# A decoder trunk's matmuls in groups of eight and of four columns: the groups of four are placed elsewhere behind the heads' products and at the begin of a step

## The chip, the cores and the metric

One NeuronCore of a Trainium2 chip runs the whole kernel. The metric is the device time of one execution in microseconds, as the median of several runs. Engines are named as in the profile: PE is TensorE (matmuls; PEld its weight loads), DVE is VectorE, ACT is ScalarE, POOL is GpSimd, SP is SyncE.

## What is computed

The reference is a decoder trunk with one layer (`DEPTH = 1`), for 256 rows of 4096 in float32: RMSNorm, stick-breaking attention with 32 heads of 128 and a SiLU gate, the residual, and a last RMSNorm.

```python
proj = rms_norm(x, norm_attn) @ w_in          # (256, 4096) @ (4096, 16384): q, k, v, gate
q, k, v, g = split(proj)
z = q @ k.T / sqrt(128)                       # per head, strictly causal
log_a = log_sigmoid(z) + suffix_sum(log_sigmoid(-z))
o = exp(log_a) @ v
h = x + (o * silu(g)) @ w_out                 # (256, 4096) @ (4096, 4096)
return rms_norm(h, final_norm)
```

The two projections are nearly all of the work.

## The kernel before

**Units and steps.** The columns of the two projections are taken in 20 units, one after the other: units 0 to 15 for `w_in`, each with the q, k, v and gate columns of two heads, and units 16 to 19 for `w_out`. A unit has 16 steps; step `s` brings 256 of the 4096 rows of the contraction. A step multiplies two halves of the rows of x (or of the heads' output), 128 each, by two halves of the contraction and two blocks of 512 weight columns. That would be eight products of 128x128 by 128x512; steps 1, 2, 4, 5, 7, 8, 10, 11, 13 and 14 of most units form them with seven, from sums and differences of the blocks (`SEVEN`, line 46, `SEVEN_PARTS`, line 83), the others and all steps of the units 0 and 16 with eight. The results add up in PSUM in up to seven banks over a unit, and `combine` (line 708) makes the columns of them at its end.

**Triples.** Each product is in float32 by three matmuls: high by high, high by low, low by high, where an operand's high part is its rounding to the narrower type that TensorE multiplies (`fp32r`) and the low part is the rest. I call the three a triple. There are 2386 triples, 7158 matmuls, in a fixed order (the list `order`). ScalarE makes the high parts of the weights (`wh`), VectorE the low parts (`wl`) and the sums; the weights come in by DMA, issued by SP and for some sums by GpSimd with an addition on the way.

**Groups of columns.** A matmul reads 512 columns of its moving operand and writes 512 of a PSUM bank. It doesn't go through them from the first to the last: the 512 are cut into short groups that lie side by side, and each of four rounds takes every fourth group. A letter for each matmul of a triple says how long a group is, `e` for eight columns and `c` for four. An `e` reads columns 0 to 7, 32 to 39, 64 to 71 and so on in its first round, a `c` 0 to 3, 16 to 19, 32 to 35. The moving operand and the bank are cut alike, so the result is the same in either order.

```python
ROUNDS = 4                                                   # line 35
RUNS = {"e": 8, "c": 4}
BEHIND_OTHERS = ("ccc", "ecc")
IN_STEP = ("cce", "ecc", "ccc")
...
for k, (x, y) in enumerate(((ah, bh), (ah, bl), (al, bh))):  # mm3, line 812
    to, y = (t.rearrange("p (h q e) -> p q h e", q=ROUNDS, e=RUNS[orders[k]]) for t in (out_, y))
...
orders = "eee"                                               # product, line 1237
if since_others < len(BEHIND_OTHERS):
    orders = BEHIND_OTHERS[since_others]
elif p["i"] == 0 and k == 0:
    orders = IN_STEP[p["s"] % len(IN_STEP)]
since_others += 1
```

So a triple is `eee` unless it is one of the first triples behind the heads' products, or the first of its step. In the kernel before, step 0 (3, 6, ...) begins with `cce`, step 1 (4, 7, ...) with `ecc`, step 2 (5, 8, ...) with `ccc`.

**The heads' products.** The attention of the two heads of unit `u` runs while unit `u + 1` is multiplied. A head puts five small pieces of work between the triples (`head`, line 823, and the function behind it): the transposes of its q and k (four matmuls), the scores (five), the scan (four, with 384 columns first), the transposes of the gate (two), and the product with v (four). That makes 160 places where TensorE leaves the triples. Each is issued by `ten` (line 344), which sets the counter `since_others` to zero, so the triples behind it are counted from there. Ahead of the scan stand the scores of the same head by some 30 matmuls of the projection; in between ScalarE makes `f` of the scores `z`, and `fh`, and VectorE `fl`.

**The order of the work.** It is laid down when the program is built. The class `Plan` (line 112) plays the kernel through with a cost for each instruction (a triple counts 666 ns whatever its letters) and issues the instructions of each engine in the order that comes out. So nearly all instructions carry line 131 in the profile, the line of the helper that records them; they are told apart by their tiles. `acc<-wh,sh` is a matmul into a bank with the stationary operand `sh` (from x; `oh` from the heads' output) and the weights' part `wh`; `sl`, `ol` and `wl` are low parts. The letters don't show in the profile; which triple a matmul belongs to follows from its place in the order.

Of the kernel before, what the change touches and what calls it, by code (L numbers as in the profile page):

```python
# [33 lines left out]

ROUNDS = 4
RUNS = {"e": 8, "c": 4}
BEHIND_OTHERS = ("ccc", "ecc")
IN_STEP = ("cce", "ecc", "ccc")
WARM, IDLE = 10, 640


# [206 lines left out]
def kernel(  # L248
# [988 lines left out]
    def product(n, k):  # L1237
# [4 lines left out]
        orders = "eee"  # L1242
# [5 lines that stand above are left out]
# [89 lines left out]
```

## Time and profile before

| | before |
|---|---|
| median of 3 runs | 1713.17 us (1711.64 to 1714.27) |
| profiled execution | 1711.9 us, its span 1710.2 us |
| granted TensorE clock, mean | 0.996 |
| PE busy | 1690.5 us, 7776 matmuls |
| DVE busy | 1608.5 us (94%) |
| ACT busy | 1202.4 us (70%) |
| matmuls of the triples | 7158, of them 1471 in groups of four |

How to read it: the profile is one execution, and its times count from the first instruction of the span. The duration of a matmul in the timeline (0.38 us and more) overlaps the next one's; what one costs is seen from one start to the next. A row of the timeline gives start, duration, engine, line, operation and tiles; a row ends with `x2` where two instructions of one kind were merged. A row of the view by stretches gives the stretch, its length, the busy time of TensorE, the matmuls touched, the granted clock, the DMA share and GB/s.

### The profile page before, as it was taken

To read this page: it belongs to the slowest core of one execution; us is meant where nothing else is said; L and a number is where in the kernel's file an instruction comes from. 1 tells how busy PE (TensorE), PEld (TensorE's weight loads), DVE (VectorE), ACT (ScalarE), POOL (GpSimd) and SP (SyncE) were. 2 spreads that over 40 slices of the span, in tenths; PEclk is the share of its full clock that TensorE was granted. 3 is DMA by queue.
4 is the path that set the end of the run, shared out by engine and by line. 5 is a ranking of instruction groups with operands and counts; after the bars stand their busy time and mean duration, and the time that the engine had idled before them with its cause. 6 is when DMAs were issued, how large, how long until landed. Compare 5 with 4: busy or idle time off the path is not lost. (4 is left out here: it accounts for less than half of the span.)

```text
span 1710.2 us, 25109 instructions
## 1 busy us (share of the span) xinstructions
PE 1690.5 (99%) x7776; PEld 1416.8 (83%) x7776; DVE 1608.5 (94%) x2025; ACT 1202.4 (70%) x1633; POOL 325.7 (19%) x400
## 2 busy tenths in 40 slices
PE   9999999999999999999999999999999999999996
PEld 7888888888888888888888888888888888888785
DVE  8889999999999999999999999999999987999996
ACT  8986767676767676767676768676767765656564
POOL 0012222122222222221212121222222112122110
PEclk9999999999999999999999999999999999999998
DMA  9978887978787979787979797878788977889794
GB/s 350 326 196 245 228 246 219 253 212 259 206 266 196 271 195 274 195 270 201 264 205 260 208 256 214 249 215 247 224 240 230 290 248 234 256 240 280 208 307 174
DMA packets 248439, 412.78 MB, mean 241 GB/s; under 512 B 28016, under 2 KB 72560, under 8 KB 248304
## 3 DMA queue, kind: packets, MB, share of 16 engines
q1 hardware_dynamic: 194544, 354.24, 62.2%
q0 software_dynamic: 53472, 56.65, 20.4%
q8 instruction: 61, 1.00, 0.2%
q14 instruction: 74, 0.61, 0.1%
q10 hardware_dynamic: 288, 0.28, 0.0%
HBM read 402.93 MB, written 8.13 MB: 240 GB/s over the span
## 5 line engine op out<-in xcount | busy, mean ns | idle before, releaser
L131 ACT CAST wh<-raw 128x1024 fp32r<-128x1024 f32 (+1 forms) x989 | 918.9, 970 | 371.7 <-PE acc L131 169.8
L131 DVE TENSOR_TENSOR wl<-raw,wh 128x1024 fp32r<-128x1024 f32 (+1 forms) x815 | 975.5, 1218 | 64.1 <-ACT wh L131 27.7
L131 PE MATMUL acc<-wh,sh 128*128 128x512 f32 x2048 | 775.9, 391 | 1.1 <-ACT wh L131 1.1
L131 PE MATMUL acc<-wh,sl 128*128 128x512 f32 x1898 | 729.1, 384 | 0.9 <-DVE sl L131 0.9
L131 PE MATMUL acc<-wl,sh 128*128 128x512 f32 x1748 | 670.1, 383 | 0.2 <-DVE wl L131 0.2
L131 POOL DMA_DIRECT2D raw<-in_w_in_dram x300 | 259.1, 958 | 1029.3 <-DMA raw<-in_w_in_dram 367.2
L131 PEld LDWEIGHTS acc<-wh,sh 128*128 128x128 f32 x2048 | 384.2, 188 | 79.5 <-DVE qk_sb L131 4.9
L131 PEld LDWEIGHTS acc<-wh,sl 128*128 128x128 f32 x1898 | 355.8, 187 | 68.5 <-DVE sl L131 1.5
L131 PEld LDWEIGHTS acc<-wl,sh 128*128 128x128 f32 x1748 | 328.3, 188 | 56.0 <-DVE wl L131 0.5
L131 DVE TENSOR_TENSOR raw<-raw,raw 128x512 f32<-128x512 f32 x348 | 237.2, 685 | 2.5 <-DMA raw<-in_w_in_dram 0.4
L131 PE MATMUL acc<-wh,oh 128*128 128x512 f32 x512 | 193.3, 385 | 0.6 <-DVE gv_sb L131 0.6
L131 PE MATMUL acc<-wh,ol 128*128 128x512 f32 x488 | 187.5, 384 | 0.0
L131 PE MATMUL acc<-wl,oh 128*128 128x512 f32 x464 | 178.6, 385 | 2.7 <-DVE wl L131 2.7
L131 DVE TENSOR_TENSOR wh<-raw,wh 128x512 fp32r<-128x512 f32 x174 | 119.2, 685 | 1.1 <-ACT wh L131 0.7
L131 DVE TENSOR_TENSOR raw<-raw 128x512 f32<-128x512 f32 x174 | 118.9, 683 | 0.0
L131 PEld LDWEIGHTS acc<-wh,oh 128*128 128x128 f32 x512 | 96.4, 188 | 18.4 <-DVE gv_sb L131 0.9
L131 PEld LDWEIGHTS acc<-wh,ol 128*128 128x128 f32 x488 | 91.9, 188 | 16.6
L131 PEld LDWEIGHTS acc<-wl,oh 128*128 128x128 f32 x464 | 87.4, 188 | 19.6 <-DVE wl L131 3.9
L131 POOL DMA_DIRECT2D raw<-in_w_out_dram x48 | 41.5, 970 | 181.1 <-DMA raw<-in_w_out_dram 67.5
L131 ACT ACTIVATE f<-f 128x384 f32<-128x384 f32 x96 | 50.4, 525 | 3.0
L131 POOL DMA_DIRECT2D p<-spill x27 | 17.6, 694 | 86.8 <-DVE ol L131 49.8
L131 DVE SCALAR_TENSOR_TENSOR gv_sb<-acc,scalars,gv_sb 128x512 f32<-128x512 f32 x45 | 33.5, 744 | 0.0
(83 smaller groups left out, 753.9 us busy)
## 6 DMA issues: line engine op xcount, KB each, us to landing
raw<-in_w_in_dram SPq DMA_DIRECT2D x1024, 256.0 KB, 4.4
raw<-in_w_out_dram SPq DMA_DIRECT2D x256, 256.0 KB, 4.2
raw<-in_w_in_dram POOLq DMA_DIRECT2D x300, 128.0 KB, 5.1
p<-spill POOLq DMA_DIRECT2D x27, 256.0 KB, 4.2
raw<-in_w_out_dram POOLq DMA_DIRECT2D x48, 128.0 KB, 5.0
xr<-in_x_dram SPq DMA_DIRECT2D x16, 256.0 KB, 5.3
xres<-in_x_dram SPq DMA_DIRECT2D x16, 256.0 KB, 5.4
out_dram<-h SPq DMA_DIRECT2D x16, 256.0 KB, 2.9
```

Of the source, the lines that this page charges most:

```text
L131: return self.tc.keep_in_program_order(getattr(self.engine, name)(*args, **kw))
```

## The change

Two constants are altered, and nothing else:

```diff
-BEHIND_OTHERS = ("ccc", "ecc")
-IN_STEP = ("cce", "ecc", "ccc")
+BEHIND_OTHERS = ("ccc", "ecc", "eee", "cce", "eee", "eee", "ecc")
+IN_STEP = ("cce", "ecc")
```

Behind the heads' products the first two triples keep their letters. The third is `eee` even where a step begins, the fourth is `cce`, the fifth and sixth are `eee` even where a step begins, and the seventh is `ecc`. A step that begins later than that starts with `cce` if its number is even and with `ecc` if it is odd; before, the three kinds went round by the step's number. By the code, of the 7158 matmuls 1515 are then in groups of four, in place of 1471. 82 triples turn from `eee` to `cce` behind the heads' products; of the 98 triples that were `ccc` at a step's begin none stays so, but for those that are also the first behind the heads' products.

## The prediction

> **What bounds the kernel now.** I read the page first, then the list of waits for TensorE alone, then the busy time by stretches, and last the timeline of TensorE around single steps. The profiled execution took 1711.9 us, 1710.2 of them its span.
>
> ```profile
> span 1710.2 us, 25109 instructions
> ...
> PE 1690.5 (99%) x7776; PEld 1416.8 (83%) x7776; DVE 1608.5 (94%) x2025; ACT 1202.4 (70%) x1633; POOL 325.7 (19%) x400
> ...
> PEclk9999999999999999999999999999999999999998
> ```
>
> The reader is to see that TensorE is busy from end to end at full clock. The waits agree: the longest entry among those of TensorE is this one, 2.9 us in 4 waits, one of them 2.2 us.
>
> ```profile
> PE acc L131 <- DVE wl L131: 2.9, 4, 2.2
> ```
>
> So TensorE sets the time, and the change alters nothing but the order in which its matmuls read their columns. The question is what one matmul costs. Three neighbouring steps of unit 0, 24 matmuls each, show it: step 7 (`ecc`), step 8 (`ccc`), step 9 (`cce`). Columns: stretch, its length, busy time, matmuls touched, granted clock, DMA share, GB/s.
>
> ```profile
> 45.31:50.59 5.28, 5.28 (x25) 1.00 1.04 378
> 50.59:56.10 5.51, 5.51 (x26) 1.00 0.72 233
> 56.10:61.42 5.32, 5.32 (x26) 1.00 0.96 336
> ```
>
> Step 7 is 5.28 / 24 = 0.220 us a matmul, step 8 is 0.2296, at the same clock and with TensorE never idle. The groups of instructions in the first two stretches show the same in the mean duration of one matmul, 382 against 390 ns:
>
> ```profile
> L131 PE MATMUL acc<-wh,sl 128*128 128x512 f32 x9 | 3.4, 382 | 0.0
> ...
> L131 PE MATMUL acc<-wh,sl 128*128 128x512 f32 x9 | 3.5, 390 | 0.0
> ```
>
> Only the first three matmuls of step 8 are in groups of four; the other 21 are in groups of eight, as in step 7, and still take 0.23. So the triple wholly in fours does not cost by itself: it puts TensorE into a **wide stretch** of about 0.230 us a matmul, which lasts until a later pair of fours (the `cce` of step 9: 5.32, 0.04 over 24 times 0.220) brings back the **narrow stretch** of 0.220. I count every term below as wide minus narrow. One matmul then carries 0.0096 us, and 1 us of gain is about 104 matmuls.
>
> **The change part by part.** By the code, no instruction is added or removed: 2386 triples stay where they are, and of 7158 matmuls those in fours go from 1471 to 1515. No DMA, wait or queue moves. (The change's words say that the fourth and seventh triple carry one product in groups of four; in the diff `cce` and `ecc` carry two, and I go by the diff.) Steps now begin with `cce` (even) or `ecc` (odd) unless fewer than seven triples lie behind the heads' products. A pair in a narrow stretch costs nothing in step 7 above. The eight steps 8 to 15 of unit 6, 177 matmuls, begin at the first of these rows and end at the second:
>
> ```profile
> 561.22 0.38 PE L131 MATMUL acc<-wh,sh 128*128 128x512 f32 x1
> ...
> 600.24 0.38 PE L131 MATMUL acc<-wh,sh 128*128 128x512 f32 x1
> ```
>
> 39.02 less 177 x 0.220 = 0.08 us, for five pairs and three `ccc`. I take 0.007 for a pair (ends 0 and 0.013) and 0.02 for a `ccc` that leaves the stretch narrow.
>
> *Unit 0.* Steps 1 to 15 run from the first row to the second:
>
> ```profile
> 13.30 0.38 PE L131 MATMUL acc<-wh,sh 128*128 128x512 f32 x1
> ...
> 93.64 0.60 PE L131 MATMUL tr<-ident,qk_sb 128*128 128x128 f32 x4
> ```
>
> 80.34 less 360 x 0.220 = 1.14 us too much; four of its five `ccc` (steps 5, 8, 11, 14) start a wide stretch. After: 15 pairs, 0.10. Gain 1.04.
>
> *Step 5 of units 2 to 15.* It has 18 matmuls ahead of a head's scan, begins with `ccc`, and is wide each time; the first and the last of the 14:
>
> ```profile
> 206.67 0.38 PE L131 MATMUL acc<-wh,sh 128*128 128x512 f32 x1
> ...
> 210.80 0.34 PE L131 MATMUL z<-fh,neg_tri 128*128 128x384 f32 x1
> ...
> 1305.98 0.38 PE L131 MATMUL acc<-wh,sh 128*128 128x512 f32 x1
> ...
> 1310.10 0.34 PE L131 MATMUL z<-fh,neg_tri 128*128 128x384 f32 x1
> ```
>
> 4.125 less 18 x 0.220 = 0.165. It is now the seventh triple and gets `ecc`: 0.007. Gain 14 x 0.158 = 2.2.
>
> *Step 1.* Here the third triple behind the scores is the step's `ecc`, and what follows is wide up to the scan, 24 matmuls, in 12 of the units 2 to 15; the first and the last:
>
> ```profile
> 184.38 0.39 PE L131 MATMUL acc<-wh,sh 128*128 128x512 f32 x1
> ...
> 189.88 0.33 PE L131 MATMUL z<-fh,neg_tri 128*128 128x384 f32 x1
> ...
> 1283.66 0.39 PE L131 MATMUL acc<-wh,sh 128*128 128x512 f32 x1
> ...
> 1289.16 0.33 PE L131 MATMUL z<-fh,neg_tri 128*128 128x384 f32 x1
> ```
>
> 5.50 less 5.28 = 0.22. After the change that third triple is `eee`. The same heads' product of the second head has an `eee` there already. In unit 6 its third triple begins at the first row, the fourth at the second, step 5 at the third:
>
> ```profile
> 542.26 0.39 PE L131 MATMUL acc<-wh,sh 128*128 128x512 f32 x1
> ...
> 542.96 0.38 PE L131 MATMUL acc<-wh,sh 128*128 128x512 f32 x1
> ...
> 544.94 0.38 PE L131 MATMUL acc<-wh,sh 128*128 128x512 f32 x1
> ```
>
> The third triple takes 0.70 (0.04 over), the nine matmuls behind it 1.98, which is narrow. So an `eee` there recovers by itself. What the new `cce` does to the fourth triple, directly behind such a third, no row shows. Its ends: nothing, or a wide stretch up to the pair of the seventh, nine matmuls at 0.0096 and 0.04 to end it, 0.13. I take 0.02, nearer to nothing, because the recovery is over at 542.96. Together 0.04 + 0.02 + two pairs, 0.08; gain 12 x 0.14 = 1.7.
>
> *Unit 16 and the last unit.* Unit 16's step 8 is the first two rows (5.51, 0.23 over); its step 14 is alike and half of step 2 is. In the last unit, step 14 and the step behind it, 45 matmuls, run from the third row to the fourth.
>
> ```profile
> 1408.87 0.38 PE L131 MATMUL acc<-wh,oh 128*128 128x512 f32 x1
> ...
> 1414.38 0.39 PE L131 MATMUL acc<-wh,oh 128*128 128x512 f32 x1
> ...
> 1670.93 0.38 PE L131 MATMUL acc<-wh,oh 128*128 128x512 f32 x1
> ...
> 1681.16 0.38 PE L131 MATMUL acc<-wh,oh 128*128 128x512 f32 x1
> ```
>
> 0.56 and 10.23 - 9.90 = 0.33; less the pairs, 0.5 and 0.3.
>
> *The other `ccc` at a step's begin.* Some 61 that stay narrow become pairs: 61 x 0.013 = 0.8.
>
> *What is added behind the heads' products.* 82 triples go from `eee` to `cce` and 50 (of `eee` or `ccc`) to `ecc`, of which 24 are counted in step 1 and 14 in step 5; 32 other third triples lose their pair. (94 - 32) x 0.007 = 0.4 lost. Also, how the first two triples behind a scan run depends on what ran ahead of it. Behind step 2's `ccc` six matmuls take 1.38 us (first two rows), behind the wide step 5 they take 1.43 (last two):
>
> ```profile
> 528.63 0.44 PE L131 MATMUL acc<-wh,sh 128*128 128x512 f32 x1
> ...
> 530.01 0.38 PE L131 MATMUL acc<-wh,sh 128*128 128x512 f32 x1
> ...
> 549.58 0.44 PE L131 MATMUL acc<-wh,sh 128*128 128x512 f32 x1
> ...
> 551.01 0.38 PE L131 MATMUL acc<-wh,sh 128*128 128x512 f32 x1
> ```
>
> The first may lose 0.05 and the second gain it, 14 times each: I take nothing, ends -1.4 and +1.4.
>
> **Sum:** 1.04 + 2.2 + 1.7 + 0.5 + 0.3 + 0.8 - 0.4 = 6.1 us off the profiled 1711.9, so 1705.8. The median of the runs, 1713.17, lies 1.3 above that execution; from it 1707.1.
>
> What hides behind TensorE must also be early enough. In unit 6 VectorE ends the second head's `fl` at 547.44 and the scan that reads it begins at 549.06: 1.6 us in hand, against 0.165 taken.
>
> ```profile
> 546.89 0.55 DVE L131 TENSOR_TENSOR fl<-f,fh 128x384 fp32r<-128x384 f32 x1
> ...
> 549.06 0.34 PE L131 MATMUL z<-fh,neg_tri 128*128 128x384 f32 x1
> ```
>
> The one long wait is near the end, where the chain of waits (first two rows) runs through the loads and VectorE:
>
> ```profile
> 1582.43 2.81 DMA raw<-in_w_out_dram
> ...
> 1588.98 2.28 DVE wl L131 x2
> ...
> 1591.30 0.80 PE L131 MATMUL acc<-wl,oh 128*128 128x512 f32 x1 [2.19 <-DVE wl L131]
> ...
> 1591.00:1596.00 5.00, 4.70 (x14) 0.66 0.99 297
> ```
>
> It costs 2.2 us and a clock of 0.66 behind it. A gain made long before moves that whole stage forward; only what units 17 and 18 gain (under 0.3 us) could be lost there.
>
> [...]
>
> **The rivals.**
> *Cost goes by the number of fours.* Each four costs 0.0096 wherever it stands; 44 more are 0.4 us: 1713.6. For it: the wide steps begin with the most fours. Against: step 7 has two fours and costs 5.28, and 21 eights of step 8 are wide. [...] Chance 0.05.
> *The gain becomes a wait.* TensorE reaches the heads' products sooner and waits there for VectorE and ScalarE; the 3.9 us of steps 1 and 5 are lost, 2.2 stay: 1711.0. Against: the 1.6 us in hand. Chance 0.07.
> *The fourth triple's pair starts a wide stretch, and the seventh's doesn't end it* (slower). Three heads' products a unit have six or more triples behind the fourth, 45 places in units 1 to 15; 24 wide matmuls each, up to the next step's begin, cost 0.23: 10.4 lost against 6.1, 1717.5. It decides from 0.14 us a place, 14 wide matmuls. For it: step 1 shows that a pair at the wrong place behind the heads' products does just this. Against: there the pair stood a triple earlier, before the recovery. Chance 0.06.
> The forecast has 0.82.
>
> **The numbers.** 1707.1 us. The unknown costs (a pair 0 to 0.013 at some 220 places, the fourth triple, the triples behind a scan) make 3 us to the good and 4 to the bad if all fall one way; they are independent, so I take half, 4 to 7.6 us of gain. With 1.3 us for the spread of the runs (1711.64 to 1714.27) to either side the forecast's own range is 1704 to 1710.5. Up to 1711 it takes in most of the second rival. A measurement tells 0.2%, 3.4 us, from no change: faster 0.82, within 0.12, slower 0.06.
>
> **What would show it.** In the profile after: steps 5, 8, 11 and 14 of unit 0 at 5.28 to 5.30 each; step 5 of units 2 to 15 at 3.96 to 3.98 ahead of the scan; step 1 at 5.31 to 5.40; TensorE's matmuls of `acc` some 6 us less in all, with the same waits. I am wrong if step 1 stays at 5.5, if a step that begins with a pair out of a narrow stretch turns wide, or if TensorE's waits grow by microseconds.

## The result, and the profile after

The kernel after takes 1708.36 us (median of 9 runs, 1706.34 to 1710.01); the kernel before, run beside it, takes 1711.86 (9 runs, 1710.44 to 1714.27). The ratio is 0.9976, with a 95% interval of 0.9967 to 0.9984: **faster by 0.24%, some 4.1 us**. The profiled execution took 1706.34 us against 1711.9.

The head of the page after (span, busy time, granted clock) and the longest wait of TensorE:

```profile
span 1704.6 us, 25109 instructions
...
PE 1685.6 (99%) x7776; PEld 1415.9 (83%) x7776; DVE 1607.4 (94%) x2025; ACT 1202.5 (71%) x1633; POOL 325.0 (19%) x400
...
PEclk9999999999999999999999999999999999999998
```

```profile
PE acc L131 <- DVE wl L131: 2.8, 4, 2.1
```

TensorE's busy time fell by 4.9 us (1690.5 to 1685.6) and its waits are as before: 4 waits for `wl`, 2.8 us, one of them 2.1. So nothing that was gained was lost again by waiting.

**The steps of unit 0.** Steps 7, 8 and 9 by stretches, in the kernel after (the first two columns are the stretch and its length; then the busy time of PE, PEld, DVE, ACT and POOL, each with the instructions touched; then the granted clock, the DMA share and GB/s):

```profile
45.29:50.59 5.30, 5.30 (x26) 4.50 (x24) 4.90 (x8) 5.24 (x11) 0.00 (x0) 1.00 1.00 364
50.59:55.88 5.29, 5.29 (x25) 4.50 (x24) 4.55 (x8) 4.75 (x11) 0.00 (x0) 1.00 0.75 222
55.88:61.17 5.29, 5.29 (x25) 4.50 (x24) 4.85 (x10) 5.26 (x13) 0.00 (x0) 1.00 0.94 310
```

Step 8 was 5.51 and is 5.29. Steps 1 to 15 run from the first of the next rows to the second, 79.40 us against 80.34:

```profile
13.55 0.38 PE L131 MATMUL acc<-wh,sh 128*128 128x512 f32 x1
...
92.95 0.38 PE L131 MATMUL tr<-ident,qk_sb 128*128 128x128 f32 x2
```

**Step 5 of unit 6,** from its first matmul to the scan, in the kernel after:

```profile
543.55 0.38 PE L131 MATMUL acc<-wh,sh 128*128 128x512 f32 x1
...
547.51 0.34 PE L131 MATMUL z<-fh,neg_tri 128*128 128x384 f32 x1
```

3.96 us against 4.12 before, and 3.96 is 18 x 0.220; the other 13 units show the same 3.96.

**Step 1,** in two neighbouring units of the kernel after. Three rows each: the third triple behind the scores (the step's begin), the fourth, and the scan. First unit 5, then unit 6:

```profile
436.93 0.39 PE L131 MATMUL acc<-wh,sh 128*128 128x512 f32 x1
...
437.59 0.38 PE L131 MATMUL acc<-wh,sh 128*128 128x512 f32 x1
...
442.23 0.34 PE L131 MATMUL z<-fh,neg_tri 128*128 128x384 f32 x1
```

```profile
521.20 0.39 PE L131 MATMUL acc<-wh,sh 128*128 128x512 f32 x1
...
521.90 0.39 PE L131 MATMUL acc<-wh,sh 128*128 128x512 f32 x1
...
526.73 0.34 PE L131 MATMUL z<-fh,neg_tri 128*128 128x384 f32 x1
```

Unit 5 takes 5.30, unit 6 takes 5.53, no less than before. They part at the third triple. In unit 5 it takes 0.66, three narrow matmuls, and the pair of the fourth does no harm. In unit 6 it takes 0.70, and everything from there to the scan is wide; step 1 at 5.5 was one of the prediction's own signs of being wrong. Over the units 2 to 15, eight are like unit 6 (2, 4, 6, 7, 9, 11, 13, 15) and six like unit 5. This is the step that did not come as forecast.

**A part that is not the change's.** The last matmul of the triples starts 5.56 us earlier than before (first row before, second after):

```profile
1696.82 0.39 PE L131 MATMUL acc<-wh,ol 128*128 128x512 f32 x1
```

```profile
1691.26 0.40 PE L131 MATMUL acc<-wh,ol 128*128 128x512 f32 x1
```

Of this, 1.49 us lie in unit 18, behind the one long wait. Before, the clock behind it was 0.66; after, it is 1.00 although the wait is nearly as long:

```profile
1587.74 0.49 PE L131 MATMUL acc<-wl,oh 128*128 128x512 f32 x1 [2.08 <-DVE wl L131]
...
1587.80:1592.80 5.00, 5.00 (x22) 4.12 (x23) 4.65 (x6) 0.76 (x1) 0.00 (x0) 1.00 1.02 364
```

Over all 13 profiled executions, one of each kernel, the drop came behind waits of 1.86 to 2.26 us in six and did not come behind waits of 1.70 to 2.09 us in seven (last section), so I don't count it as a gain of the change. Without it the two traces differ by 4.1 us, as the medians' ratio has it. How often the drop came in the executions without a profile isn't known: their mean clocks, 0.996 to 0.998 for the kernel after, are too coarse to tell.

### The profile page after: what moved, and what is told of

The parts are those of the page before. It is cut to its first block, busy times and chain, and to the rows that moved or that the text cites. A ratio compares the mean times of both kernels' runs of the same rounds, so it can differ in the third digit from the quotient of the medians.

```text
span 1704.6 us, 25109 instructions
## 1 busy us (share of the span) xinstructions
PE 1685.6 (99%) x7776; PEld 1415.9 (83%) x7776; DVE 1607.4 (94%) x2025; ACT 1202.5 (71%) x1633; POOL 325.0 (19%) x400
## 4 chain that ended last, share of the span: by engine, by line
PE 94%; DVE 3%; issue 1%; DMA 1%; ACT 0%; SPq 0%; DVEq 0%; ACTq 0%
PE acc L131 90%; PE z L131 2%; PE o L131 2%; DVE wl L131 1%; PE tr L131 1%; DVE h L131 0%; DVE raw L131 0%; ACT wh L131 0%; DMA raw<-in_w_in_dram 0%; DMA raw<-in_w_out_dram 0%; DMA xres<-in_x_dram 0%; DVE wh L131 0%; DVE gv_sb L131 0%; SPq L131 0%; DVE scalars L131 0%
```

## The experiments

Theory A: a stretch is narrow or wide, whatever it holds; the fourth triple's pair of fours, directly behind a third triple that is still wide, keeps the stretch wide. Theory B: the third triple's own `eee` is what keeps step 1 wide. Theory C: the time goes by the number of fours. Each edit is given against the kernel after; behind the first diff a line that replaces one of the two constants is shown alone. The columns: median of the runs, ratio to the kernel before with its interval, matmuls in fours.

| kernel | us (runs) | ratio to before | fours |
|---|---|---|---|
| after | 1708.36 (9) | 0.9976 [0.9967, 0.9984] | 1515 |
| e1_no_fourth | 1705.5 (5) | 0.9959 [0.9946, 0.9971] | 1349 |
| e2_steps_alone | 1707.44 (8) | 0.9971 [0.9961, 0.9981] | 1373 |
| e3_behind_alone | 1711.44 (11) | 0.9996 [0.9987, 1.0005] | 1597 |
| e4_pair_at_fifth | 1705.67 (5) | 0.9961 [0.9949, 0.9974] | 1485 |
| e5_steps_in_eights | 1709.35 (12) | 0.9987 [0.9976, 0.9997] | 805 |
| e6_steps_ecc | 1706.48 (5) | 0.9967 [0.9955, 0.9979] | 1313 |
| e7_all_eights | 1754.93 (4) | 1.0248 [1.0235, 1.0261] | 0 |
| e8_all_fours | 1722.21 (4) | 1.0058 [1.0045, 1.0071] | 7158 |
| e9_pairs_where_wide | 1705.81 (5) | 0.9957 [0.9945, 0.9969] | 899 |
| e10_one_pair | 1708.0 (12) | 0.9977 [0.9967, 0.9987] | 809 |
| e11_no_seventh | 1707.26 (6) | 0.9971 [0.9959, 0.9982] | 1479 |

**The fourth triple without its pair (`e1_no_fourth`).**

```diff
-BEHIND_OTHERS = ("ccc", "ecc", "eee", "cce", "eee", "eee", "ecc")
+BEHIND_OTHERS = ("ccc", "ecc", "eee", "eee", "eee", "eee", "ecc")
```

> The changed kernel with its fourth triple behind the heads' products back to eee; the rest stays. Theory A (the pair at the fourth triple falls into a recovery and starts a wide stretch that the seventh's pair doesn't end): step 1 of units 2 to 15 falls from 5.5 us to 5.3 to 5.36, nothing else moves, so about 2.5 us less than the changed kernel, some 6.5 us less than before (ratio 0.996). Theory B (the third triple's eee itself leaves step 1 wide, the pair has no part in it): step 1 stays at 5.5 and the time that of the changed kernel, ratio 0.9976. Theory C (cost by the number of fours, 1349 in place of 1515): 166 x 0.0096 = 1.6 us less than the changed kernel, spread over all units, with step 1 still wide.

1705.5 us, by the ratios 2.9 below the kernel after, where A had 2.5. Step 1 of unit 6 in this kernel, the same three rows (third triple, fourth, scan):

```profile
520.75 0.39 PE L131 MATMUL acc<-wh,sh 128*128 128x512 f32 x1
...
521.45 0.38 PE L131 MATMUL acc<-wh,sh 128*128 128x512 f32 x1
...
526.07 0.34 PE L131 MATMUL z<-fh,neg_tri 128*128 128x384 f32 x1
```

The third triple takes 0.70, as wide as in the kernel after; but now an `eee` stands behind it, and the 21 matmuls to the scan take 4.62, narrow. In 13 of the 14 units the third triple is wide and step 1 is 5.32; in the other it is narrow and step 1 is 5.29. So a wide third triple is followed by narrow ones when the next is an `eee`, and B is refuted; it is the pair directly behind it that stops the recovery. A's "nothing else moves" is a miss: unit 16, where the same list stands, takes 0.7 us less as well.

**The pair one triple later (`e4_pair_at_fifth`).**

```diff
+BEHIND_OTHERS = ("ccc", "ecc", "eee", "eee", "cce", "eee", "ecc")
```

> The changed kernel with the fourth triple's cce moved one triple back, to the fifth, where the recovery is over. A: a pair in a narrow stretch costs 0 to 0.013 us wherever it stands, so step 1 falls to 5.3 to 5.37 as without the pair and the time is within 0.5 us of the kernel without it: 6.5 us less than before, ratio 0.996. If any pair within seven triples of the heads' products starts a wide stretch, step 1 stays at 5.5 and the ratio at 0.9976.

1705.67 us, as fast as with no such pair. The three rows in unit 6:

```profile
521.23 0.39 PE L131 MATMUL acc<-wh,sh 128*128 128x512 f32 x1
...
521.93 0.38 PE L131 MATMUL acc<-wh,sh 128*128 128x512 f32 x1
...
526.57 0.34 PE L131 MATMUL z<-fh,neg_tri 128*128 128x384 f32 x1
```

Again a third triple of 0.70, then 4.64 for 21 matmuls, the pair among them: 0.02 over. The same pair costs 0.2 us at the fourth place and 0.02 at the fifth. What counts is not the pair but the stretch that it falls into.

**The two halves of the change.** Only the steps' begins (`e2_steps_alone`):

```diff
+BEHIND_OTHERS = ("ccc", "ecc")
 IN_STEP = ("cce", "ecc")
```

> Only the steps' begins of the change: no step begins with ccc, behind the heads' products stands what stood there before. A: unit 0 falls by 0.7 to 1.0 us, step 5 becomes narrow (3.96 to 3.98 us ahead of the scan), step 1 stays wide because the step's ecc is again the third triple; 4.5 us less than before, ratio 0.9974. C: 1373 fours, 98 less than before, 0.9 us less, ratio 0.9995.

Only the triples behind the heads' products (`e3_behind_alone`):

```diff
 BEHIND_OTHERS = ("ccc", "ecc", "eee", "cce", "eee", "eee", "ecc")
+IN_STEP = ("cce", "ecc", "ccc")
```

> Only the change behind the heads' products; the steps begin with cce, ecc, ccc in turn as before. A: unit 0 as before (steps 5, 8, 11, 14 at 5.51), step 1 wide by the fourth triple's pair, step 5's ccc is replaced by the seventh's ecc and becomes narrow; the added pairs and the recoveries that they break cost what step 5 gives: within 1 us of before, ratio 0.9995 to 1.0006. My prediction's working would have given 2.2 + 1.7 - 0.4 = 3.5 us less, ratio 0.998. C: 1597 fours, 1.2 us more.

Step 8 of unit 0, with the steps alone and then with the list behind the heads' products alone:

```profile
51.05:56.34 5.29, 5.29 (x25) 4.50 (x24) 4.55 (x8) 4.67 (x10) 0.00 (x0) 1.00 0.68 216
```

```profile
50.79:56.30 5.51, 5.51 (x25) 4.51 (x24) 4.56 (x8) 4.88 (x11) 0.00 (x0) 1.00 0.70 228
```

The steps alone give 1707.44, the whole gain of the change; step 5 is 3.96 in all 14 units. Step 1, which I expected to stay wide, is 5.50 in five of them and 5.30 to 5.32 in nine. From a unit's begin to the scan of its step 1 all triples but the last have the letters of the kernel before, where 12 of the 14 were wide: the letters close by don't decide alone whether that stretch is wide. The part behind the heads' products alone gives 1711.44, no difference that can be measured: step 5 is 3.96 there too, since the list gives its first triple an `ecc` in place of the `ccc`, but step 1 is 5.51 in eight units, unit 0 is wide again in every third step, and unit 16 loses 0.45 us. So the kernel after owes its gain to the steps, and the list behind the heads' products adds nothing: what it gains in step 5 the steps' change brings as well, and the rest it loses at the fourth triple.

**The seventh triple without its pair (`e11_no_seventh`).**

```diff
+BEHIND_OTHERS = ("ccc", "ecc", "eee", "cce")
```

> As the kernel after, but the seventh triple behind the heads' products is eee: the fourth triple's pair alone. Theory A with the fourth triple's pair as the culprit of step 1: step 1 stays at 5.5 in about half of the units, step 5 stays at 3.96 because it begins with no ccc; the time is that of the kernel after within 1 us, 1707.5 to 1709.5. Rival (the seventh's ecc is what keeps step 1 wide, since it stands in the middle of it): step 1 at 5.3 in all units, 1706. Rival (the seventh's pair is needed to bring a narrow stretch back): step 1 wide in more than 8 of 14 units and other long stretches behind the heads' products wide, 1711 or more.

1707.26, a little under the range that I expected, and not to be told from the kernel after. Step 1 is 5.52 or 5.53 in five units and 5.28 to 5.30 in nine; as in the kernel after, it is wide exactly in those whose third triple takes 0.70. What the seventh's pair is worth shows in step 1 of unit 16, which is longer. There the wide stretch of the fourth triple runs from the first row to the second in the kernel after, and in the kernel without the seventh's pair likewise:

```profile
1365.32 0.39 PE L131 MATMUL acc<-wh,oh 128*128 128x512 f32 x1
...
1369.46 0.39 PE L131 MATMUL acc<-wh,oh 128*128 128x512 f32 x1
```

```profile
1365.03 0.39 PE L131 MATMUL acc<-wh,oh 128*128 128x512 f32 x1
...
1372.63 0.38 PE L131 MATMUL acc<-wh,oh 128*128 128x512 f32 x1
```

4.14 us for 18 matmuls in the first, 7.60 for 33 in the second, both 0.230 each. The seventh's pair does end the wide stretch, but narrow matmuls come only three triples behind it; the step's pair in the second kernel takes as long. In step 1 of the units 2 to 15 the scan comes first, so there it ends nothing.

**All in eights (`e7_all_eights`), and all in fours (`e8_all_fours`).**

```diff
+BEHIND_OTHERS = ()
+IN_STEP = ("eee",)
```

> Every matmul of a triple in groups of eight, behind the heads' products too. A: the fours behind the heads' products end wide stretches that those products leave; without any, a wide stretch lasts from one heads' product to the next and through the rest of a unit, so up to 7158 less unit 0's 384 matmuls at 0.0096: as much as 60 us more than before, with unit 0 at 5.28 a step. C: no fours, 14 us less than before.

```diff
+BEHIND_OTHERS = ()
+IN_STEP = ("ccc",)
...
-        orders = "eee"
+        orders = "ccc"
```

> Every matmul of a triple in groups of four: the cost of a four by itself. [...] A: a long run of fours has nothing to be switched by; unit 0 at one spacing from step to step, 5.28 if the length of a group doesn't matter, and in all between 60 us more and 7 us less than before, so this tells A and C apart only together with the kernel wholly in eights.

Step 7 of unit 0, in eights and then in fours:

```profile
46.50:52.04 5.54, 5.54 (x26) 4.52 (x24) 3.87 (x6) 3.85 (x9) 0.00 (x0) 1.00 0.99 362
```

```profile
46.38:51.84 5.46, 5.46 (x26) 4.50 (x25) 4.08 (x7) 4.42 (x10) 0.00 (x0) 1.00 1.04 382
```

No fours at all is 2.5% slower, all fours 0.6%. By C, at 0.0096 for each four, the kernel without any would be 14 us faster than before, and the one in fours, with 5687 more, 55 us slower; by the ratios they are 42 and 10 us slower: C is refuted from both sides. With eights alone nearly the whole kernel is wide (0.231 a matmul), unit 0 too, for which A had 5.28 a step: another miss. With fours alone the steps of unit 0 lie between (5.42 to 5.46, some 0.227), and from step 6 of unit 18 on a step of 24 matmuls takes 5.36 (0.223). So the two values 0.220 and 0.231 are those of the eights, and the few fours among them are what brings them back to the lower one.

**Steps in eights (`e5_steps_in_eights`).**

```diff
+BEHIND_OTHERS = ("ccc", "ecc")
+IN_STEP = ("eee",)
```

> No fours at the steps' begins at all; ccc and ecc stay behind the heads' products as before. A (a four costs by the stretch that it starts or ends, and a recovery left alone ends by itself): unit 0 at 5.28 a step, step 1 at 5.30 to 5.34, step 5 at 3.96, 7 to 8.5 us less than before, ratio 0.9955. If the pairs at the steps' begins are needed to end wide stretches that come from the heads' products, those now last for whole steps or units: more than before. C: 805 fours, 666 less than before, 6.4 us less, ratio 0.9963, in every unit alike.

1709.35, a miss: 2.2 us less than before by the ratio, where I expected 7 to 8.5. The trace shows why, although it is of one of the slower executions (1713.03 us). A step in unit 0, one in unit 17, one in unit 19, all 24 matmuls in eights:

```profile
46.76:52.29 5.53, 5.53 (x25) 4.52 (x24) 3.87 (x6) 3.77 (x9) 0.00 (x0) 1.00 0.98 359
...
1479.95:1485.23 5.28, 5.28 (x26) 4.50 (x24) 5.28 (x8) 4.27 (x6) 1.72 (x2) 1.00 0.82 226
1623.27:1628.81 5.54, 5.54 (x26) 4.53 (x25) 5.54 (x10) 3.36 (x4) 2.23 (x4) 1.00 1.06 267
```

The same instructions run at 5.53 in one unit and at 5.28 in another. Unit 0 begins wide and stays so for all its steps (2.9 us over the kernel before); unit 17 is narrow to the last; the long wait in unit 18 turns the stretch wide, and unit 19, which has no heads' products, stays wide to its end (3.0 over). Of the units 2 to 15 all but one run 0.33 to 0.47 us below the kernel before (unit 13 is 0.1 above). In the units 0, 17 and 19 eights carry on whatever stretch they meet: they neither start one nor end one.

**One order for every step (`e6_steps_ecc`).**

```diff
+BEHIND_OTHERS = ("ccc", "ecc", "eee", "eee")
+IN_STEP = ("ecc",)
```

> ccc, ecc, eee, eee behind the heads' products, and every step that begins later than that begins with ecc. A: nothing is broken in its recovery, and a pair that is there ends what is wide: 7 to 8.5 us less than before, ratio 0.9955, the same as without fours at the steps within 1 us. C: 1313 fours, 1.5 us less than before, ratio 0.9991, and 4.9 us more than with the steps in eights.

1706.48, 5.7 us below the kernel before by the ratio, less than expected; step 1 is 5.29 to 5.33 in every unit, unit 0's steps are 5.28 from step 2 on. It is 2.9 us faster than the kernel with its steps in eights, where A had the two alike and C had it 4.9 slower: pairs at the steps' begins are worth something. Its interval overlaps that of the kernel without the fourth's pair, so no gain by alternating `cce` and `ecc` is seen.

**Pairs only where a wide stretch runs (`e9_pairs_where_wide`).** Behind the heads' products `("ccc", "ecc")`, and in `product`:

```diff
-        elif p["i"] == 0 and k == 0:
+        elif p["i"] == 0 and k == 0 and p["u"] in (0, 18, 19):
```

> Behind the heads' products only the ccc and the ecc of the kernel before; steps begin in eights, but with the pairs (cce, ecc) in the units 0, 18 and 19 alone. In the trace of the kernel whose steps all begin in eights the units 2 to 12 and 15 ran 0.37 to 0.47 us below the kernel before, and only unit 0 (+2.9), unit 18 behind its long wait (+0.9) and unit 19 (+3.0) were above. Theory A (two stretches: a pair is wanted only where a wide stretch runs, and is a small cost elsewhere): unit 0's steps at 5.28 to 5.30, units 2 to 15 as without pairs, in all 8 to 9 us below before, near 1703.5. Theory A2 (the pairs are needed in every unit, and the loss of 3 us in unit 0 is one of the start of the kernel): unit 0 stays at 5.54 a step, 1708 to 1710. Theory C (cost by the number of fours): 45 more fours than with steps in eights, no faster than that, 1709 to 1710.

Step 8 of unit 0 and step 13 of unit 19:

```profile
50.66:55.95 5.29, 5.29 (x26) 4.50 (x24) 4.54 (x8) 4.67 (x10) 0.00 (x0) 1.00 0.79 265
1641.59:1646.88 5.29, 5.29 (x25) 4.50 (x24) 5.26 (x7) 3.66 (x5) 0.00 (x0) 1.00 0.80 305
```

1705.81: unit 0's steps are 5.28 to 5.32 from step 2 on and unit 19 narrow, as A has it. The 94 fours more than in the kernel with steps in eights (not 45, as the expectation counts) make it faster, against C. The gain is 7.4 us by the ratio, below the 8 to 9 expected. It is the fastest profiled execution of all (1702.71 us), but no better by the medians than the kernel without the fourth's pair.

**One pair in a whole unit (`e10_one_pair`).**

```diff
+        elif p["i"] == 0 and k == 0 and p["u"] in (0, 19) and p["s"] == 8:
```

> As the last, but a single pair in unit 0, at the begin of step 8 (cce or ecc by the order of steps), and a single one in unit 19, at its step 8. Theory A (a stretch stays as it is until something ends it): steps 2 to 7 of unit 0 at 5.54 each, step 8 at about 5.4, steps 9 to 15 at 5.28; unit 19 wide up to its step 8 if the long wait of unit 18 has made it wide, narrow behind; in all about half of what e5 loses in those units comes back: near 1706. Theory A2 (each step needs its pair): only step 8 changes, 0.2 us a unit, 1709. Theory C: no change against e5, 1709.

1708.0. Steps 7, 8 and 9 of unit 0; step 8 holds the only pair:

```profile
48.69:54.23 5.54, 5.54 (x26) 4.52 (x24) 3.87 (x6) 3.52 (x8) 0.00 (x0) 1.00 0.87 322
54.23:59.56 5.33, 5.33 (x26) 4.50 (x25) 4.41 (x8) 4.84 (x10) 0.00 (x0) 1.00 0.48 151
59.56:64.84 5.28, 5.28 (x26) 4.50 (x25) 5.02 (x10) 5.25 (x13) 0.00 (x0) 1.00 0.99 338
```

Seven steps at 5.53 to 5.54, one at 5.33, and steps 9 to 14 at 5.28 without another pair: **one pair ends a wide stretch, and eights alone then stay narrow**. The single pair of unit 19 does the same. There a wait in step 4 had turned the stretch wide; steps 9, 8 and 14 (the order in that unit), of which step 8 holds the pair:

```profile
1660.08:1665.62 5.54, 5.54 (x26) 4.52 (x24) 4.70 (x5) 3.00 (x5) 1.23 (x2) 1.00 1.06 270
1665.62:1670.95 5.33, 5.33 (x26) 4.50 (x24) 3.92 (x6) 2.22 (x3) 0.00 (x0) 1.00 1.01 371
1670.95:1676.23 5.28, 5.28 (x26) 4.50 (x24) 4.10 (x4) 2.48 (x4) 0.00 (x0) 1.00 0.55 169
```

In both units the matmuls are narrow from the second triple behind the pair on. Behind the heads' products, where the fourth triple is `eee`, the stretch turns narrow just as late, two triples behind the `ecc` of the second one. So it may be that `ecc`, and not the `eee`, that ends it there: in the kernel wholly in eights, which lacks it, step 1 is 5.53 or 5.54 in 12 of 14 units. No run takes out the `ecc` alone.

The time is higher than the 1706 expected, and unit 17 shows what happened in the profiled execution (1711.51 us). Two matmuls came late; then step 6, ahead of them, and step 9, behind:

```profile
1486.51 0.40 PE L131 MATMUL acc<-wh,oh 128*128 128x512 f32 x1
1486.84 0.50 PE L131 MATMUL acc<-wl,oh 128*128 128x512 f32 x1
1487.18 0.40 PE L131 MATMUL acc<-wh,ol 128*128 128x512 f32 x1
```

```profile
1479.25:1484.53 5.28, 5.28 (x25) 4.50 (x24) 5.28 (x8) 3.81 (x7) 1.70 (x2) 1.00 0.78 235
1495.03:1500.56 5.53, 5.53 (x26) 4.52 (x25) 4.72 (x6) 3.43 (x4) 1.73 (x2) 1.00 1.05 253
```

From 1486.51 two matmuls start 0.33 apart, 0.23 us late in all, and with nothing to end it the stretch stays wide through the rest of unit 17, which ends 2.1 us over the kernel before, and on into unit 18. Without the fourth's pair and without the seventh's a delay came at the same place, and there the stretch is narrow again behind the next step's begin, which holds a pair. The kernels with steps in eights and with single pairs also scatter widely, 1707.23 to 1714.65 and 1704.77 to 1712.08 in 12 runs each, against 1710.08 to 1715.92 in 18 runs of the kernel before; that such accidents make the scatter is argued, not shown.

## Why the prediction was right, and where it was wrong

The forecast was 1707.1 and the measured time 1708.36, inside the range. That it came so near is in part luck: the kernel before ran at 1711.86 in the new runs, 1.3 us below the median that the forecast started from, and this made up for a part of the gain that didn't come. The gain is the better measure: 6.1 us were forecast, 4.1 were measured, by the ratio, and by the traces without the 1.49 us of unit 18. Term by term, from the traces:

| term | forecast | measured |
|---|---|---|
| unit 0, steps 1 to 15 | 1.04 | 0.94 |
| step 5 of 14 units | 2.2 | 2.2 |
| step 1 | 1.7 | 0.6 |
| unit 16 | 0.5 | 0.05 |
| last unit | 0.3 | 0.5 |
| other steps, what is added, and the rest | 0.8 - 0.4 | -0.2 |

Of the last row -0.24 is step 0 of unit 0 (7.49 us against 7.25), at the start of the kernel, which takes 7.25 to 9.84 us in the 13 traces; without it the row is nothing, in place of 0.4. (The "32 other third triples" of the prediction are by the code 16 third, 15 fifth and one sixth; the count, and so the sum, is right.)

- **What bounds the kernel, and wide and narrow stretches:** right. The time moved by what the matmuls' spacing moved, and no wait grew by microseconds. The runs in eights and in fours show the two stretches more plainly than the kernel before did: 0.220 and 0.231 us for the same instructions.
- **Unit 0 and step 5:** right in mechanism and size.
- **Step 1: the step that failed** is "I take 0.02, nearer to nothing, because the recovery is over at 542.96." At 542.96 an `eee` stood, and it was this `eee` that went narrow; the third triple's 0.70 ahead of it was wide throughout. I read the end of the third triple as the end of the recovery. Where the third triple is wide, a pair in place of that `eee` holds the stretch wide: in step 1 of 8 of 8 such units of the kernel after and of 5 of 5 without the seventh's pair. Where it is narrow, the pair is free, in 6 of 6 and 9 of 9. Over all 50 heads' products of the kernel after with at least six triples behind them, a pair behind a narrow third stays narrow at 37 of 37 places, and one behind a wide third is wide at 11 of 13. One triple later the pair costs some 0.02 in step 1 of all 14 units, whatever the third triple.
- **The upper end of that cost** was too low as well: "a wide stretch up to the pair of the seventh, nine matmuls". The seventh's pair works three triples late, behind the scan, so where it is wide step 1 costs 0.25 over narrow and not 0.13.
- **Unit 16** lost its 0.5 to the same thing: its steps 8 and 14 came to 5.29 as forecast, but its step 1 rose from 5.29 to 5.47, step 6 from 5.32 to 5.42 and step 13 from 5.28 to 5.39. Three of the 11 places are there, ahead of or in these steps.
- **The third rival** (the fourth's pair starts a wide stretch) was therefore a true mechanism at 11 places rather than 45. It got a chance of 0.06 as a whole, with a price for all places or none; it should have stood in the sum as a part of them.
- **The waits:** as forecast, none came. In unit 6 `fl` is ready 1.5 us ahead of the scan in the kernel after (this row ends at 546.03; the scan is at 547.51):

```profile
545.48 0.55 DVE L131 TENSOR_TENSOR fl<-f,fh 128x384 fp32r<-128x384 f32 x1
```

- **The rival by the number of fours** is out by the two extremes. The kernel with runs of four columns is 33 us faster than the one with runs of eight, and a step of eights alone takes 5.28 or 5.53.

The best versions are the kernel after without the fourth's pair (0.9959 [0.9946, 0.9971]), the one with that pair at the fifth triple (0.9961 [0.9949, 0.9974]) and the one with pairs only in three units (0.9957 [0.9945, 0.9969]). They can't be told apart; their ratios lie 0.0015 to 0.0019 below that of the kernel after, with intervals that just overlap. The cause that the runs show is which stretch follows which letters; what sets the third triple wide or narrow from one unit to the next stays open, as does what a wide stretch is in the hardware.

## What to carry to other kernels

Where the same instruction has two durations at the same clock with no wait, look for a state that lasts: compare what ran ahead of it, not what it is, and price an edit by whether it starts, ends or merely meets such a stretch. Price it for each entry that the trace shows: a mechanism that holds at some of the places belongs in the sum with their share, and a row in which something recovers says nothing of what happens when the instruction that did the recovering is replaced.

## What the runs showed of the hardware

- Matmuls of 512 columns in groups of eight, at a granted clock of 1.00 and with TensorE never idle, start 0.220 or 0.231 us apart, and either goes on for whole units of some 80 us. The start of the kernel, the long wait in unit 18 and a delay of 0.23 us have each been followed by the wide one (steps of 5.53 and 5.54 in the units 0 and 19 with the steps in eights, of 5.53 in unit 17 with single pairs), but not always: a delay of 0.55 us in step 5 of unit 18, with the steps in eights, left the stretch narrow (5.28 for the next step). A triple wholly in fours at a step's begin started one in four of five places of unit 0 before (5.51 a step). A pair of matmuls in fours ends one, some one to three triples later (with single pairs three steps take 5.54, 5.33 and 5.28, the pair at the begin of the second), but at the fourth triple behind a wide third it mostly keeps it going (11 of 13 places of the kernel after). The long wait in unit 18 can end one too: in the kernel with single pairs, behind 1.70 us, the steps are narrow (5.28 for the next one of 24 matmuls); in the kernel wholly in eights, behind a wait of 1.70 us as well, they stay wide (5.54). Why is open.
- Slow matmuls behind a wait of about 2 us come or not. Before, the matmuls behind the 2.19 us wait start 0.43 us apart (first two rows), about twice 0.22, at a granted clock of 0.50 from 1591.30 to 1594.00; so they do behind 2.26 us with the steps in eights and, from the fifth matmul on, behind 2.03 us with the steps of the change alone (last rows: the clock over 5 us is 0.66). In the kernel after, behind 2.08 us, they do not (a clock of 1.00 over 5 us). It costs some 1.5 us, by the 1.49 us of unit 18.

```profile
1591.89 0.63 PE L131 MATMUL acc<-wh,ol 128*128 128x512 f32 x1
1592.32 0.63 PE L131 MATMUL acc<-wh,oh 128*128 128x512 f32 x1
```

```profile
1588.76 0.79 PE L131 MATMUL acc<-wl,oh 128*128 128x512 f32 x1 [2.26 <-DVE wl L131]
```

```profile
1586.86 0.49 PE L131 MATMUL acc<-wl,oh 128*128 128x512 f32 x1 [2.03 <-DVE wl L131]
...
1586.86:1591.86 5.00, 5.00 (x15) 3.98 (x16) 4.71 (x6) 0.70 (x1) 0.00 (x0) 0.66 1.05 363
```

The length of the wait doesn't decide alone: 1.86 us of idleness were followed by slow matmuls in one execution (the kernel wholly in fours), and 2.09 us were not in another (the pair at the fifth triple).
